# A two-layer decoder step in high and low parts: row sums in a tile of their own, plain blocks' low parts on VectorE, three wide PSUM tiles, and the last projection's first products begun early

## The chip, the cores and the metric

The kernel runs on one core of a Trainium2 chip. The metric is the device time of one execution in microseconds (us). Five engines work in parallel, each through its own instruction stream in order: TensorE (PE; its weight loads are shown as PEld), VectorE (DVE), ScalarE (ACT), GpSimd (POOL) and SyncE (SP, which here only issues DMAs). They meet through semaphores.

## The reference

One inference step of a decoder with two layers on 520 rows of width 1024: 512 prompt rows and 8 rows of samples. Layer 0 mixes tokens by windowed attention, layer 1 by gated linear attention. Behind each stands the same feed-forward block, on which the change bears:

```python
def conv_ffn(x, buf, w_up, conv_w, conv_b, w_down):
    T = x.shape[1]
    h = x @ w_up                                  # 1024 -> 2 * 2816
    a, u = h[..., :D_FF], h[..., D_FF:]
    ap = jnp.concatenate([buf.astype(a.dtype), a], axis=1)
    c = conv_b + sum(conv_w[j] * ap[:, j:j + T] for j in range(CONV_W))   # 3 taps
    y = (jax.nn.gelu(c, approximate=False) * u) @ w_down                  # 2816 -> 1024
    return y, ap[:, T:]
```

## The kernel before

Everything is kept transposed: 128 features on the partitions, rows in the free dimension, in two groups, a (rows 0 to 255) and b (264 rows, the samples among them). Each float32 matrix is split into a high part, rounded by ScalarE to the matmul's type, and a low part, the rest. A product is three matmuls for each 128 features: high by high, high weight by low row, low weight by high row (L216, L218 and L220 or, where all low-weight products come last, L223; L282 to L284 in a pair; L860 to L862 in the partial down projection).

Weights come in units of 128 x 1024 floats (512 KB). SyncE loads the raw unit, ScalarE writes the high part `wh` (L177 in a plain unit). The low part `wl` is made in one of two ways. VectorE subtracts: `wl = raw - wh` (L183, or L288 in `split`). Or, `low_by_dma`: ScalarE writes `-wh` into `wl` (L188) and GpSimd issues a DMA (L189) that loads the unit from memory once more and adds it. Six pairs of `wh` and `wl` slots (`WSLOTS`) and two raw buffers (`RAWS`) go round; a unit's loads are issued in program order when a slot is released.

A feed-forward block has 22 column blocks of 128 gate and 128 value columns. The first four (`PAIRED`) are **plain**: a gate unit and a value unit, each multiplied with the rows of a and of b into one-bank PSUM tiles `accp`, the convolution, the gelu, and `hprod`, the gated product. In the other 18, the **pairs** (`ffn_pair`), gate and value together are computed by a Strassen-like scheme with seven half products instead of eight, on sums and differences of rows (`row_sums`: `th`, `tl`) and of weights. `pair_tasks` prepares the weights in four steps: `upper` loads both raw units and splits one (L245, low part by DMA), `lower` and `sums` add halves on VectorE (L234) and split, `third` splits a half-size sum into `wh3` and `wl3`. `ffn_pair` first makes the product p1 into a one-bank tile `sc`, copies it (L806), then fills three two-bank tiles `widep`, of which VectorE (L799) and ScalarE (L812) make the merged gate and value. Between most pairs stands a unit of the partial down projection (`ffn_down2`), two more wide tiles, which VectorE adds into x (L865, L867). `WIDES` two-bank tiles are there, and four banks for the small tiles (`sc` two of them). The last six blocks' down projection is the ordinary `ffn_down`, eight units, each for a and then for b.

The source gives work in the order of `order()` and `load_next`, which stops while six slots are live, or while two of the `half` tiles are. A scheduler then settles each engine's own sequence, so a matmul can stand far ahead of its place in the source.

Of the kernel before, what the change touches and what calls it, by code (L numbers as in the profile page):

```python
# [11 lines left out]
F32 = mybir.dt.float32  # L12
F32R = mybir.dt.float32r
# [4 lines left out]
PSUM = bass.MemoryType.PSUM  # L18
DRAM = bass.MemoryType.DRAM

P = 128
# [25 lines left out]

PAIRED = 4
ACCS = 4
WIDES = 2  # L50

WARM = 8

# [30 lines left out]
def in_turn(rows):  # L84

    return rows.rearrange("p t j -> p j t")
# [10 lines left out]
class Net:  # L97
    def __init__(self, tc, ctx, I, O):
        self.tc, self.nc, self.I, self.O = tc, tc.nc, I, O
        self.groups = [Group(0), Group(1)]  # L100
        self.stack = ctx
        pool = lambda name, bufs=1, **kw: ctx.enter_context(tc.tile_pool(name=name, bufs=bufs, **kw))
        self.const = pool("const")
        self.act = pool("act")
        self.raw = pool("raw", RAWS)
        self.wts = pool("wts", WSLOTS)
        self.ln = pool("ln")
        self.mps = pool("mps", space=PSUM)
        self.open_acc()
        self.dram = pool("dram", 2, space=DRAM)  # L110
        nc = self.nc
        c = self.const
        self.par = c.tile([P, NPAR], F32, name="par")
        self.ident = c.tile([P, P], F32, name="ident")
        self.ones_a = c.tile([P, P], F32, name="ones_a")
        nc.gpsimd.memset(self.ones_a, 1.0 / D)
        self.eps = c.tile([P, 2], F32, name="eps")
        nc.gpsimd.memset(self.eps[:, 0:1], NORM_EPS)
        nc.gpsimd.memset(self.eps[:, 1:2], 1.0)
        for i, g in enumerate(self.groups):  # L120
            s = [P, KD, g.n]
            g.x = self.act.tile(s, F32, name=f"x_{g.name}")


            if i == 0:
                s = [P, KD, 2, 2, g.n // 2]
                g.xs = self.act.tile(s, F32R, name=f"xs_{g.name}")
                g.hs = self.act.tile(s, F32R, name=f"hs_{g.name}")
                g.xh, g.xl = (g.xs[:, :, :, q] for q in range(2))
                g.hh, g.hl = (g.hs[:, :, :, q] for q in range(2))  # L130
                continue
            s = [P, KD, 2, g.n // 2]
            g.xs = g.hs = None
            g.xh = self.act.tile(s, F32R, name=f"xh_{g.name}")
            g.xl = self.act.tile(s, F32R, name=f"xl_{g.name}")
            g.hh = self.act.tile(s, F32R, name=f"hh_{g.name}")
            g.hl = self.act.tile(s, F32R, name=f"hl_{g.name}")
        self.units = []
        self.w = {}
# [7 lines left out]
    def close(cm):  # L147
        cm.__exit__(None, None, None)

    def open_acc(self):  # L150
        self.acc_cm = self.tc.tile_pool(name="acc", bufs=ACCS, space=PSUM)
        self.acc = self.acc_cm.__enter__()

    def open_wide(self):
        self.acc_cm = self.tc.tile_pool(name="wide", bufs=WIDES, space=PSUM)
        self.acc = self.acc_cm.__enter__()

    def wide(self):
        return self.acc.tile([P, 2, 512], F32, name="widep")


    def load_unit(self, u, pieces=1, late=False):
        src, nt = self.units[u][0], self.units[u][1]
        nc = self.nc
        if nt == 0:
            return self.load_rank(u)
        down = self.units[u][2] == self.ffn_down2
        r = (self.pp if down else self.raw).tile([P, KD * P], F32, name="raw")
        h, l = (self.wts.tile([P, KD * P], F32R, name=name) for name in ("wh", "wl"))
        n = nt * P // pieces  # L170
        for c in (slice(i * n, (i + 1) * n) for i in range(pieces)):
            nc.sync.dma_start(out=r[:, c], in_=src[:, c])
            if late:
                self.spawn(self.parts(u, h[:, c], l[:, c], r[:, c]), 1)
                continue
            if u >= HIACT:
                nc.scalar.activation(h[:, c], r[:, c], AF.Copy)  # L177
            else:
                nc.gpsimd.tensor_scalar(h[:, c], r[:, c], 1.0, 0.0, op0=ALU.mult, op1=ALU.add)
            if self.units[u][2] in (self.ffn_gate, self.ffn_value, self.ffn_down2):  # L180
                self.low_by_dma(l[:, c], h[:, c], src[:, c])
            else:
                nc.vector.tensor_tensor(l[:, c], r[:, c], h[:, c].bitcast(F32), op=ALU.subtract)  # L183
        self.w[u] = (h, l)
# [41 lines left out]
    def pair_tasks(self, u):  # L226


        nc, half = self.nc, KD * P // 2
        lo, hi = slice(0, half), slice(half, KD * P)  # L230
        src0, src1 = self.units[u][0]
        W, T = {}, {}
        self.w[u] = W
        add = lambda o, x, y: nc.vector.tensor_tensor(o, x, y, op=ALU.add)  # L234
        slot = lambda: [self.wts.tile([P, KD * P], F32R, name=name) for name in ("wh", "wl")]

        def keep(h, l, first, second):
            W[first], W[second] = (h[:, lo], l[:, lo]), (h[:, hi], l[:, hi])

        def upper():  # L240
            r1, r0 = (self.raw.tile([P, KD * P], F32, name="raw") for _ in range(2))
            nc.sync.dma_start(out=r1, in_=src1)
            nc.sync.dma_start(out=r0, in_=src0)
            h, l = slot()
            nc.scalar.activation(h, r0, AF.Copy)  # L245
            self.low_by_dma(l, h, src0)
            keep(h, l, "a11", "a12")
            T.update(r0=r0, r1=r1)

        def lower():  # L250
            r0, r1 = T["r0"], T["r1"]
            s = T["s"] = self.pp.tile([P, half], F32, name="sum3")
            add(s, r1[:, lo], r0[:, lo])
            add(r1[:, lo], r1[:, lo], r1[:, hi])
            h, l = slot()
            self.split(h, l, r1)
            keep(h, l, "s1", "a22")

        def sums():
            r0, r1 = T["r0"], T["r1"]  # L260
            add(r0[:, lo], r1[:, lo], r0[:, lo])
            add(r0[:, hi], r0[:, lo], r0[:, hi])
            h, l = slot()
            self.split(h, l, r0)
            keep(h, l, "s2", "s4")

        def third():
            h, l = (self.pp.tile([P, half], F32R, name=name, bufs=2) for name in ("wh3", "wl3"))
            self.split(h, l, T["s"])
            W["s3"] = h, l  # L270

        return [("live", upper), ("live", lower), ("live", sums), ("half", third)]
# [71 lines left out]
    def ln_end(self, g, i, last=False):  # L344
# [72 lines left out]
            self.norm = self.slot + HOLD, self.exp, v.ins, xl.ins, self.next_phase() + 1  # L417
        if i % 2 == 0:
            if g.i:
                self.spawn(self.row_sums(i), 1)  # L420
            return
        for m in range(KD):
            yield 1 if m else LATEB
# [6 lines left out]
    def row_sums(self, i):  # L430
# [11 lines left out]
            v.tensor_tensor(self.t1[k], a.x[:, k, 0:256], b.x[:, k, 0:256], op=ALU.subtract)  # L442
            self.shift(b, i, half + k)
        yield 1
        r = wide(self.raw.tile([P, KD * P], F32, name="raw"))
        for k in range(half):
            v.scalar_tensor_tensor(r[:, k], self.t1[k], -1.0, b.x[:, half + k, 0:256], op0=ALU.mult, op1=ALU.subtract)
            self.shift(a, i, half + k)
# [330 lines left out]
    def ffn_pair(self, u, layer, j, q):  # L779
# [4 lines left out]
        if j == PAIRED:  # L784
            self.row_sum1()
            self.close(self.cp_cm)
            self.cp, self.cp_cm = self.open(f"merged{layer}")
            self.m = [self.cp.tile([P, 2, 2 + NT], F32, name=f"merged{i}") for i in range(2)]
            self.c = [self.cp.tile([P, 2, NT - 256], F32, name=f"conv{i}") for i in range(2)]
            for t in self.m:  # L790
                nc.gpsimd.memset(t[:, 0, 0:2], 0.0)
            self.close(self.acc_cm)
            self.open_wide()
        half = KD // 2
        part = lambda g, ks: (g.xh[:, ks], g.xl[:, ks])
# [4 lines left out]
        M, C = self.m[j % 2], self.c[j % 2]  # L800
        both = lambda x: x.unsqueeze(1).broadcast_to([P, 2, x.shape[-1]])
        g, h = M[:, 0], M[:, 1, 2:]
        p1 = self.mtile("sc")
        self.half_product(p1, W["a11"], part(a, lo), n)
        v = self.ln.tile([P, NT - 256], F32, name="nv")[:, :n]
        nc.scalar.copy(v, p1[:, :n])  # L806
# [32 lines left out]
        if j == NF - 1:  # L839
            nc.scalar.dma_start(out=self.O["conv_p"][layer], in_=self.nconv_p)  # L840
            nc.scalar.dma_start(out=self.O["conv_s"][layer], in_=self.nconv_s)
            for cm in (self.cp_cm, self.pp_cm, self.fp_cm, self.acc_cm):
                self.close(cm)
            self.open_acc()

    def ffn_down2(self, u, layer, part, i):
# [20 lines left out]
                nc.vector.tensor_tensor(x, x, ps[:, :, :n], op=ALU.add)  # L867
        self.release()

    def ffn_down(self, g, u, layer, part, m):  # L870
        nc = self.nc
        ps = self.product(g, u, g.hh, g.hl)
        yield from self.ln_chunk(g, m, ps, True, last=layer == 1)
        if m == KD - 1:
            yield from self.ln_end(g, 2 * layer + 1, last=layer == 1)
# [340 lines left out]
    def load_next(self):  # L1216
        while True:
# [9 lines left out]
            if kind == "live":  # L1227
                if self.live == WSLOTS:
                    return
                self.live += 1  # L1230
            else:
                if self.half == 2:
                    return
                self.half += 1
            self.todo.pop(0)
# [6 lines left out]
    def run(self):  # L1242
# [20 lines left out]
        while self.later:  # L1263
            self.slot += 1
            self.due()
        self.close(self.acc_cm)


def build(nc, I, O):
# [115 lines left out]
```

## Time and profile before

| | |
|---|---|
| timed runs | 1193.8 us median of 2 (1192.94 and 1194.66) |
| profiled execution | 1184.46 us, span of the trace 1182.7 us |
| PE busy | 1095.6 us (93%), 9174 matmuls |
| DVE, ACT, POOL busy | 896.1 (76%), 657.5 (56%), 356.2 us (30%) |
| mean granted PE clock | 0.973 of full |
| feed-forward block of layer 0: plain blocks, pairs | 187 to 235 us, 235.5 to 504.5 us of the span |
| feed-forward block of layer 1: plain blocks, pairs | 810 to 857.7 us, 857.7 to 1128.7 us |

In a row of the chain of waits stand the engine, the line that waited, what it waited for, the total in us, how often, and the longest. In a row of the timeline stand the start in us, the duration in us, the engine, the line, the operation, the tile written, the tiles read, and in brackets the idle time ahead of the row and what ended it. A row of windows has, for each stretch, the busy us and the number of instructions of each engine, then the granted PE clock, the DMA engines' busy share and GB/s.

### The profile page before, as it was taken

The page shows a single profiled execution, that of the slowest core. Times are in us where ns is not written, and L with a number is a line of the kernel's source. Part 1 is how long each engine was busy: PE and PEld are TensorE (multiplying, and loading weights), DVE is VectorE, ACT ScalarE, POOL GpSimd, SP SyncE. Part 2 cuts the span into 40 slices and gives each one's busy share as a digit, 9 for nine tenths or more (in the row PEclk, how much of TensorE's full clock was granted, in tenths as well). Part 3 has the DMA queues.
Part 4 walks back from the last instruction along what each step waited for, and adds up shares of the span by engine and source line. Part 5 has one row for each costly group of instructions (what it writes and reads, how often), then busy time and mean ns, then how long its engine had stood idle before and what let it go on. Part 6 is the DMA issues. An engine that isn't in the chain of part 4 may idle for free. (4 is left out here: it accounts for less than half of the span.)

```text
span 1182.7 us, 23889 instructions
## 1 busy us (share of the span) xinstructions
PE 1095.6 (93%) x9174; PEld 1055.4 (89%) x9174; DVE 896.1 (76%) x1778; ACT 657.5 (56%) x1307; POOL 356.2 (30%) x565
## 2 busy tenths in 40 slices
PE   9999996899999999999999999997799999999995
PEld 8997895899999999988899999996799999999995
DVE  7897678667777777778867877778657877777776
ACT  5677456656555565445545655455655556555444
POOL 3575677211111111056211100467211111111045
PEclk9999998999999999999899999997989999999998
DMA  7562132766677776432125355331767777776412
GB/s 237 154 189 67 50 100 49 161 167 167 171 164 170 169 165 155 128 106 91 54 99 164 106 174 179 130 119 43 165 160 166 164 165 163 178 171 150 132 55 73
DMA packets 64466, 161.68 MB, mean 137 GB/s; under 512 B 7992, under 2 KB 28512, under 8 KB 64352
## 3 DMA queue, kind: packets, MB, share of 16 engines
q1 hardware_dynamic: 51536, 119.47, 31.7%
q0 software_dynamic: 10656, 38.80, 19.6%
q10 hardware_dynamic: 2160, 1.89, 0.5%
q8 instruction: 72, 1.18, 0.4%
q14 instruction: 42, 0.34, 0.1%
HBM read 147.47 MB, written 8.47 MB: 132 GB/s over the span
## 5 line engine op out<-in xcount | busy, mean ns | idle before, releaser
L177 ACT ACTIVATE wh<-raw 128x1024 fp32r<-128x1024 f32 (+2 forms) x98 | 99.3, 1013 | 79.9 <-PE widep L283 41.4
L189 POOL DMA_DIRECT2D wl<-in_w_down x32 | 27.6, 863 | 345.8 <-ACT wl L188 345.8
L216 PE MATMUL accp<-xs_a,wh 128*128 128x256 f32 x400 | 113.5, 298 | 10.9 <-ACT wh L177 9.5
L282 PE MATMUL widep<-th,wh 128*128 128x264 f32 (+1 forms) x432 | 120.0, 278 | 0.0
L283 PE MATMUL widep<-tl,wh 128*128 128x264 f32 (+1 forms) x432 | 119.9, 278 | 0.0
L284 PE MATMUL widep<-th,wl 128*128 128x264 f32 (+1 forms) x432 | 119.8, 277 | 0.0
L216 PE MATMUL accp<-xh_b,wh 128*128 128x264 f32 x400 | 115.6, 289 | 4.1 <-ACT xh_b L413 4.1
L220 PE MATMUL accp<-xh_b,wl 128*128 128x264 f32 x400 | 113.5, 284 | 0.0
L218 PE MATMUL accp<-xl_b,wh 128*128 128x264 f32 x384 | 108.5, 283 | 0.0
L218 PE MATMUL accp<-xs_a,wh 128*128 128x256 f32 x384 | 107.7, 293 | 0.0
L288 DVE TENSOR_TENSOR wl<-raw,wh 128x1024 fp32r<-128x1024 f32 x72 | 86.7, 1220 | 10.4 <-ACT wh L287 10.1
L216 PEld LDWEIGHTS accp<-xs_a,wh 128*128 128x128 f32 x400 | 81.6, 205 | 13.1 <-ACT wh L177 10.4
L183 DVE TENSOR_TENSOR wl<-raw,wh 128x1024 fp32r<-128x1024 f32 (+3 forms) x64 | 74.9, 1176 | 11.5 <-ACT wh L177 11.0
L216 PEld LDWEIGHTS accp<-xh_b,wh 128*128 128x128 f32 x400 | 77.5, 194 | 6.4 <-ACT xh_b L413 4.9
L282 PEld LDWEIGHTS widep<-th,wh 128*128 128x128 f32 x432 | 83.0, 192 | 0.0
L283 PEld LDWEIGHTS widep<-tl,wh 128*128 128x128 f32 x432 | 83.0, 192 | 0.0
L284 PEld LDWEIGHTS widep<-th,wl 128*128 128x128 f32 x432 | 82.9, 192 | 0.0
L287 ACT ACTIVATE wh<-raw 128x1024 fp32r<-128x1024 f32 x72 | 74.2, 1046 | 13.2 <-PE accp L218 5.8
L282 PE MATMUL widep<-xh_b,wh 128*128 128x264 f32 x288 | 79.8, 277 | 0.0
L283 PE MATMUL widep<-xl_b,wh 128*128 128x264 f32 x288 | 79.6, 277 | 0.0
L284 PE MATMUL widep<-xh_b,wl 128*128 128x264 f32 x288 | 79.6, 277 | 0.0
L218 PEld LDWEIGHTS accp<-xs_a,wh 128*128 128x128 f32 x384 | 78.4, 204 | 1.1 <-DVE xs_a L288 0.7
(410 smaller groups left out, 4263.7 us busy)
## 6 DMA issues: line engine op xcount, KB each, us to landing
raw<-in_w_up SPq DMA_DIRECT2D x88, 512.0 KB, 4.2
wl<-in_w_up POOLq DMA_DIRECT2D x42, 512.0 KB, 6.4
raw<-in_w_down SPq DMA_DIRECT2D x32, 512.0 KB, 4.1
wl<-in_w_down POOLq DMA_DIRECT2D x32, 512.0 KB, 6.4
raw<-in_w_gla SPq DMA_DIRECT2D x24, 512.0 KB, 3.5
raw<-in_w_mix_o SPq DMA_DIRECT2D x16, 512.0 KB, 4.4
raw<-in_w_down SPq DMA_DIRECT2D x16, 384.0 KB, 3.3
qs<-hl SPq DMA_DIRECT2D x64, 64.0 KB, 2.2
```

The lines of the kernel that those rows point to most:

```text
L177: nc.scalar.activation(h[:, c], r[:, c], AF.Copy)
L183: nc.vector.tensor_tensor(l[:, c], r[:, c], h[:, c].bitcast(F32), op=ALU.subtract)
L189: self.nc.gpsimd.dma_start(out=l, in_=src, accum_op=ALU.add)
L216: nc.tensor.matmul(o, h[:, ks], xh, start=k == 0, stop=False)
L218: nc.tensor.matmul(o, h[:, ks], xl, start=False, stop=False)
L220: nc.tensor.matmul(o, l[:, ks], xh, start=False, stop=not tail and k == nt - 1)
L282: self.nc.tensor.matmul(o, h[:, ks], rh, start=k == 0, stop=False)
L283: self.nc.tensor.matmul(o, h[:, ks], rl, start=False, stop=False)
L284: self.nc.tensor.matmul(o, l[:, ks], rh, start=False, stop=k == KD // 2 - 1)
L287: self.nc.scalar.activation(hi, src, AF.Copy)
L288: self.nc.vector.tensor_tensor(lo, src, hi.bitcast(F32), op=ALU.subtract)
```

## The change

- The raw tile of a plain unit is always one of the two of the pool `raw`. The difference of rows `r` in `row_sums`, and `r0` of `upper`, move into tiles `raw` of the pool `pp`, two of their own; `upper` issues the load of `r0` first. `row_sums` starts three slots later in place of one.
- Low parts of gate and value units are subtracted by VectorE; only `upper` and `ffn_down2` keep the DMA. Of the units that take this path, three in each layer, six negations on ScalarE and six DMAs of 512 KB on GpSimd's queue go, and six VectorE subtractions of 128x1024 come.
- `WIDES` is 3. The small tiles' banks are closed during the pairs, and p1 has two banks of its own, `onep`.
- `wh3` and `wl3` have one buffer in place of two, and `half` stops at one.
- The last down projection's first four products for a are begun together over their first five 128-feature steps (`HEADS`), and ended one by one.

```diff
-WIDES = 2
+WIDES = 3
+HEADS = 4
...
     def open_wide(self):
-        self.acc_cm = self.tc.tile_pool(name="wide", bufs=WIDES, space=PSUM)
-        self.acc = self.acc_cm.__enter__()
+        self.acc, cm0 = self.psum("wide", WIDES)
+        self.one, cm1 = self.psum("one", 2)
+        self.psum_cms = cm1, cm0
...
-        down = self.units[u][2] == self.ffn_down2
-        r = (self.pp if down else self.raw).tile([P, KD * P], F32, name="raw")
+        r = self.raw.tile([P, KD * P], F32, name="raw")
...
-            if self.units[u][2] in (self.ffn_gate, self.ffn_value, self.ffn_down2):
+            if self.units[u][2] == self.ffn_down2:
                 self.low_by_dma(l[:, c], h[:, c], src[:, c])
             else:
                 nc.vector.tensor_tensor(l[:, c], r[:, c], h[:, c].bitcast(F32), op=ALU.subtract)
...
         def upper():
-            r1, r0 = (self.raw.tile([P, KD * P], F32, name="raw") for _ in range(2))
+            r0 = self.pp.tile([P, KD * P], F32, name="raw", bufs=2)
+            r1 = self.raw.tile([P, KD * P], F32, name="raw")
+            nc.sync.dma_start(out=r0, in_=src0)
             nc.sync.dma_start(out=r1, in_=src1)
-            nc.sync.dma_start(out=r0, in_=src0)
...
-            h, l = (self.pp.tile([P, half], F32R, name=name, bufs=2) for name in ("wh3", "wl3"))
+            h, l = (self.pp.tile([P, half], F32R, name=name) for name in ("wh3", "wl3"))
...
-                self.spawn(self.row_sums(i), 1)
+                self.spawn(self.row_sums(i), 3)
...
-        r = wide(self.raw.tile([P, KD * P], F32, name="raw"))
+        r = wide(self.pp.tile([P, KD * P], F32, name="raw", bufs=2))
...
-        p1 = self.mtile("sc")
+        p1 = self.one.tile([P, 512], F32, name="onep")
...
     def ffn_down(self, g, u, layer, part, m):
-        ps = self.product(g, u, g.hh, g.hl)
+        end = self.units[u][1] - 1
+        if g.i == 0 and m == 0:
+            self.heads = [self.acc.tile([P, 512], F32, name="accp") for _ in range(HEADS)]
+            for i, ps in enumerate(self.heads):
+                self.down_steps(g, u + i, ps, range(end))
+        if g.i == 0 and m < HEADS:
+            ps = self.heads[m]
+            self.down_steps(g, u, ps, [end])
+            ps = ps[:, :g.n]
+        else:
+            ps = self.product(g, u, g.hh, g.hl)
...
-                if self.half == 2:
+                if self.half == 1:
```

`down_steps` issues the three matmuls of `product` for each of the given 128-feature steps.

The change moves instructions on the engines. In the rows below, those of after bear the changed file's line numbers: L177 is L186 there, L183 is L192, L188 is L197, L234 is L243, L245 is L255, L282 to L284 are L292 to L294, L287 and L288 are L297 and L298, L767 is L777, L799 is L809, L806 is L816, L812 is L822 and L829 is L839.

First, ScalarE where the plain blocks of layer 0 begin: `aext` and `conv` belong to the convolution, `th` is the high part of the row sums, `wh` and `wl` are the parts of the next plain unit. Before:

```order
L754 COPY aext<-accp 128x264
L767 ACTIVATE conv<-conv 128x256
L756 ACTIVATE conv<-accp,par 128x256
L287 ACTIVATE th_2735<-raw 128x8x128
L177 ACTIVATE wh<-raw 128x1024
L287 ACTIVATE hs_a<-hprod 128x2x128
L767 ACTIVATE conv<-conv 128x264
L188 ACTIVATE wl<-wh 128x1024
```

After:

```order
L764 COPY aext<-accp 128x264
L777 ACTIVATE conv<-conv 128x256
L766 ACTIVATE conv<-accp,par 128x256
L186 ACTIVATE wh<-raw 128x1024
L297 ACTIVATE th_2734<-raw 128x8x128
L297 ACTIVATE hs_a<-hprod 128x2x128
L777 ACTIVATE conv<-conv 128x264
```

The high part of the weights now stands ahead of the row sums' first split, and the negation is gone.

Second, PE in the pairs of layer 0, with tile numbers, around p1 of the fourth pair (`sc_3974` before, `onep_3975` after: the same product). Before, these are rows 1783 to 1788 of the engine's sequence:

```order
L283 MATMUL widep_3796<-tl0_2738,wh_3618 128x264
L284 MATMUL widep_3796<-th0_2735,wl_3619 128x264
L284 MATMUL sc_3974<-xs_a_86,wl_3692 128x256
L282 MATMUL sc_3974<-xs_a_86,wh_3691 128x256
L283 MATMUL sc_3974<-xs_a_86,wh_3691 128x256
L284 MATMUL sc_3974<-xs_a_86,wl_3692 128x256
```

After, these are rows 1877 to 1881:

```order
L872 MATMUL widep_3942<-hl_b_92,wh_3694 128x264
L873 MATMUL widep_3942<-hh_b_91,wl_3695 128x264
L292 MATMUL onep_3975<-xs_a_86,wh_3704 128x256
L293 MATMUL onep_3975<-xs_a_86,wh_3704 128x256
L294 MATMUL onep_3975<-xs_a_86,wl_3705 128x256
```

Before, p1 is cut up and stands between the wide tiles of the pair ahead of its own; after, its twelve matmuls stand together at the head of their own pair, behind the partial down projection. The first matmul on the low part `wl_3692` is row 1785 before, and on the same part (`wl_3705`) row 1881 after.

Third, ScalarE in the pairs, where that low part is made, from the copy of the first wide tile of the second pair on (`widep_3603` before, `widep_3604` after). Before:

```order
L812 COPY merged1_3386<-widep_3603 128x8
L177 ACTIVATE wh_3666<-raw_3665 128x1024
L806 COPY nv_3794<-sc_3781 128x256
L188 ACTIVATE wl_3667<-wh_3666 128x1024
L245 ACTIVATE wh_3691<-raw_3688 128x1024
L188 ACTIVATE wl_3692<-wh_3691 128x1024
L287 ACTIVATE wh3_3815<-sum3_3774 128x512
L829 ACTIVATE conv1_3388<-merged1_3386,par_78 128x512
```

After:

```order
L822 COPY merged1_3383<-widep_3604 128x8
L186 ACTIVATE wh_3694<-raw_3693 128x1024
L197 ACTIVATE wl_3695<-wh_3694 128x1024
L255 ACTIVATE wh_3704<-raw_3700 128x1024
L297 ACTIVATE wh3_3689<-sum3_3582 128x512
L197 ACTIVATE wl_3705<-wh_3704 128x1024
L839 ACTIVATE conv1_3385<-merged1_3383,par_78 128x512
```

The upper unit is split at the same place; `wh3` now stands between its high part and its negation, and is the third pair's, where it was the fourth's. With one buffer it waits for the last matmul on the `wh3` before it (row 1697 of PE's sequence, in the third wide tile of the second pair; the first one, `widep_3604`, fills rows 1627 to 1650).

More of the change, by code (lines that the diff above doesn't have):

```diff
@@ L107, in __init__ @@
         self.ln = pool("ln")
-        self.mps = pool("mps", space=PSUM)
         self.open_acc()
@@ L148, in close, with psum, close_psum @@
         cm.__exit__(None, None, None)
+    def psum(self, name, bufs=1):
+        cm = self.tc.tile_pool(name=name, bufs=bufs, space=PSUM)
+        return cm.__enter__(), cm
     def open_acc(self):
-        self.acc_cm = self.tc.tile_pool(name="acc", bufs=ACCS, space=PSUM)
-        self.acc = self.acc_cm.__enter__()
+        self.mps, cm0 = self.psum("mps")
+        self.acc, cm1 = self.psum("acc", ACCS)
+        self.psum_cms = cm1, cm0
     def open_wide(self):
-        self.acc_cm = self.tc.tile_pool(name="wide", bufs=WIDES, space=PSUM)
-        self.acc = self.acc_cm.__enter__()
+        self.acc, cm0 = self.psum("wide", WIDES)
+        self.one, cm1 = self.psum("one", 2)
+        self.psum_cms = cm1, cm0
+    def close_psum(self):
+        for cm in self.psum_cms:
+            self.close(cm)
     def wide(self):
@@ L791, in ffn_pair @@
                 nc.gpsimd.memset(t[:, 0, 0:2], 0.0)
-            self.close(self.acc_cm)
+            self.close_psum()
             self.open_wide()
@@ L841, in ffn_pair @@
             nc.scalar.dma_start(out=self.O["conv_s"][layer], in_=self.nconv_s)
-            for cm in (self.cp_cm, self.pp_cm, self.fp_cm, self.acc_cm):
+            for cm in (self.cp_cm, self.pp_cm, self.fp_cm):
                 self.close(cm)
+            self.close_psum()
             self.open_acc()
@@ L868, in ffn_down2, with down_steps @@
         self.release()
-    def ffn_down(self, g, u, layer, part, m):
-        nc = self.nc
-        ps = self.product(g, u, g.hh, g.hl)
+    def down_steps(self, g, u, ps, ks):
+        nc = self.nc
+        h, l = self.w[u]
+        o, end = ps[:, :g.n].rearrange("p (j t) -> p j t", t=2), self.units[u][1] - 1
+        for k in ks:
+            w = slice(k * P, k * P + P)
+            rh, rl = in_turn(g.hh[:, k]), in_turn(g.hl[:, k])
+            nc.tensor.matmul(o, h[:, w], rh, start=k == 0, stop=False)
+            nc.tensor.matmul(o, h[:, w], rl, start=False, stop=False)
+            nc.tensor.matmul(o, l[:, w], rh, start=False, stop=k == end)
+    def ffn_down(self, g, u, layer, part, m):
+        end = self.units[u][1] - 1
[9 more added lines that the diff above has]
+            ps = self.product(g, u, g.hh, g.hl)
         yield from self.ln_chunk(g, m, ps, True, last=layer == 1)
@@ L1265, in run @@
             self.due()
-        self.close(self.acc_cm)
+        self.close_psum()
 def build(nc, I, O):
```

## The prediction, on record before the run

> **What bounds the kernel now.** I read the page first, then the chain of waits of TensorE, then stretches of the span, then the timeline at the waits.
>
> ```profile
> PE 1095.6 (93%) x9174; PEld 1055.4 (89%) x9174; DVE 896.1 (76%) x1778; ACT 657.5 (56%) x1307; POOL 356.2 (30%) x565
> ```
>
> TensorE has the work; no other engine is near its limit over the whole. The same 9174 matmuls are issued after the change, so whatever is gained comes out of TensorE's waits and its slow clock. The chain of waits of that engine says for whom it waits:
>
> ```profile
> PE sc L284 <- DMA wl<-in_w_up: 15.6, 15, 1.7
> PE accp L216 <- ACT wh L177: 9.5, 4, 4.2
> PE widep L282 <- DVE hprod L775: 9.2, 2, 5.1
> PE accp L223 <- DMA wl<-in_w_up: 7.0, 2, 4.0
> PE accp L216 <- DVE merged L799: 4.2, 2, 2.1
> PE widep L860 <- DVE merged L799: 2.8, 4, 1.2
> ```
>
> Four of the rows lie in the feed-forward blocks' openings or at their ends (twice each, once a layer, L177 in the main), two in the pairs. The stretches give the size of each place (layer 0's plain blocks, its pairs, layer 1's pairs):
>
> ```profile
> 187.00:235.00 48.00, 34.72 (x246) 32.36 (x245) 34.15 (x69) 27.99 (x49) 22.92 (x36) 0.86 0.50 112
> 235.50:504.50 269.00, 259.42 (x2265) 256.91 (x2266) 203.25 (x339) 151.08 (x219) 37.24 (x67) 0.99 0.67 162
> 857.70:1128.70 271.00, 261.28 (x2266) 258.32 (x2266) 203.02 (x339) 150.89 (x219) 37.76 (x67) 0.99 0.67 160
> ```
>
> **Pairs: the low part that comes by DMA.** Without a wait one matmul follows another every 0.112 us: from the first to the sixth of these rows, 0.56 us in five steps. Then the engine stands.
>
> ```profile
> 268.91 0.28 PE L282 MATMUL widep<-th,wh 128*128 128x264 f32 x1
> ...
> 269.47 0.28 PE L284 MATMUL widep<-th,wl 128*128 128x264 f32 x1
> 270.48 0.38 PE L284 MATMUL sc<-xs_a,wl 128*128 128x256 f32 x1 [0.73 <-DMA wl<-in_w_up]
> ```
>
> 2266 matmuls at 0.112 are 253.8 us; the stretches are 269.0 and 271.0, so 15.2 and 17.2 us are lost. Part of it is slow clock:
>
> ```profile
> 191.40:201.40 10.00, 5.91 (x22) 5.11 (x23) 7.96 (x16) 5.98 (x9) 9.97 (x14) 0.50 0.17 53
> 208.50:211.70 3.20, 3.20 (x15) 3.20 (x16) 0.21 (x1) 1.15 (x3) 0.18 (x1) 0.50 1.07 268
> 235.80:239.00 3.20, 3.20 (x17) 3.20 (x17) 0.43 (x1) 1.01 (x2) 0.13 (x2) 0.50 0.90 256
> 857.90:863.70 5.80, 5.80 (x28) 5.80 (x29) 2.03 (x3) 1.18 (x2) 0.13 (x2) 0.50 0.46 137
> ```
>
> The first two rows belong to the opening, below. In the last two, at a clock of 0.50, 17 matmuls took 3.2 us (1.3 too much) and 28 took 5.8 us (2.7 too much). These stand behind the opening's last wait, which stays. That leaves 13.9 and 14.5 us of waits, 28.4 together, of which the first and the last row of waits name 15.6 and 2.8; the rest are steps too short for that list.
>
> Why is the low part late? The chain behind the wait at 270.48, on ScalarE and GpSimd:
>
> ```profile
> 260.80 1.06 ACT L245 ACTIVATE wh<-raw 128x1024 fp32r<-128x1024 f32 x1 [0.64 <-DMA raw<-in_w_up]
> 261.89 1.07 ACT L188 ACTIVATE wl<-wh 128x1024 fp32r<-128x1024 f32 x1
> ...
> 263.25 0.86 POOL L189 DMA_DIRECT2D wl<-in_w_up  x1 [1.93 <-ACT wl L188]
> ```
>
> From the high part to the landing it takes 270.4 less 260.8, 9.6 us, and 7.2 of them lie behind the issue. That doesn't change. What changes is when the part is asked for: the first matmul on it is row 1785 of PE's sequence before and row 1881 after, while the split stands behind the same copy of the same wide tile. 96 rows are 10.8 us. The longest wait in the list is 1.7 us, so all 15 should go, with 9 us to spare.
>
> Two things eat of that margin. Behind the split, `wh3` now stands ahead of the negation, and with one buffer it waits for row 1697. The negation and `low_by_dma` stand behind it, as does L829, which needs the third wide tile anyway. From row 1697 to row 1881 are 184 rows, 20.6 us; `wh3` (0.6 us), the negation (1.07) and issue to landing (7.2) are 8.9. It holds with 11 us. `wh3` itself is asked for 122 rows later, 13.7 us, and in the pairs without a down unit 72 matmuls, 8.1 us, after its buffer is free, against 0.61 and 0.68 us for the two halves of its split (ScalarE and VectorE, by the rows below). Bounds of the single buffer: nothing, or 1.3 us in each of 36 pairs, 47 us, if nothing hid it; I take nothing, since both leads are over six times the split.
>
> ```profile
> L287 ACT ACTIVATE wh<-sum 128x512 fp32r<-128x512 f32 x16 | 9.8, 614 | 0.0
> L288 DVE TENSOR_TENSOR wl<-sum,wh 128x512 fp32r<-128x512 f32 x16 | 10.9, 683 | 0.0
> L799 DVE TENSOR_TENSOR conv<-widep,merged 128x512 f32<-128x512 f32 x18 | 12.4, 691 | 24.1 <-PE widep L284 24.1
> ```
>
> The third wide tile gives VectorE a tile's time more (24 matmuls, 2.7 us) to read the one before it; in the last row VectorE waits for TensorE 24.1 us in this stretch, and it is busy for 203 of 269. It can take back the 2.8 us of the last row of waits, or nothing; by their place both of a layer's are the down unit behind a merge, so I count them as gone. Of the 28.4 us I leave 3 for the shortest steps, 0.1 us each, which I can't trace to a cause: **25.5 us**. Bounds: 14 (half stays) and 28.4.
>
> **Openings.** Layer 0, around the second and third plain unit:
>
> ```profile
> 194.02 0.56 ACT L756 ACTIVATE conv<-accp,par 128x256 f32<-128x256 f32 x1
> 195.29 1.14 ACT L287 ACTIVATE th<-raw 128x1024 fp32r<-128x1024 f32 x1 [0.71 <-DVE raw L447]
> 196.32 1.05 ACT L177 ACTIVATE wh<-raw 128x1024 fp32r<-128x1024 f32 x1
> 197.43 0.58 PE L216 MATMUL accp<-xs_a,wh 128*128 128x256 f32 x1 [4.09 <-ACT wh L177]
> ...
> 208.38 1.22 PE L223 MATMUL accp<-xs_a,wl 128*128 128x256 f32 x4 [4.01 <-DMA wl<-in_w_up]
> ```
>
> `wh` stands behind the row sums' `th`, which waits for VectorE. After, it stands ahead of it: it can begin at 194.6 and end at 195.6, so TensorE goes on **1.8 us** earlier. The low part then comes from VectorE, 1.3 us behind it (below), long before TensorE has done the high products: the wait of **4.0 us** is gone, and with it the slow stretch behind it, 15 matmuls in 3.2 us, **1.5**. Against this: the slow clock of the first stall lasts past 201.4 in any case (the row from 191.40), so starting 1.8 earlier puts some eight matmuls more into it (0.9), and the next unit's low part, third in VectorE's queue, comes some 0.6 late. Layer 0: 1.8 + 4.0 + 1.5 - 0.9 - 0.6 = **5.8 us**. In layer 1 the chain of waits of that stretch (810 to 858 us) has the same two, and no slow stretch follows the second: 1.8 + 3.0 - 0.9 = **3.9**.
>
> ```profile
> PE accp L216 <- ACT wh L177: 4.2, 1, 4.2
> PE accp L223 <- DMA wl<-in_w_up: 3.0, 1, 3.0
> ```
>
> On the price of it bear these rows:
>
> ```profile
> L183 DVE TENSOR_TENSOR wl<-raw,wh 128x1024 fp32r<-128x1024 f32 x42 | 53.8, 1283 | 7.4 <-ACT wh L177 6.9 <-PE accp L220 0.3
> L188 ACT ACTIVATE wl<-wh 128x1024 fp32r<-128x1024 f32 x74 | 78.1, 1055 | 0.7
> 196.59 1.69 POOL L428 TENSOR_SCALAR x_a<-x_a,par 128x256 f32<-128x256 f32 x1
> 196.80 1.21 DVE L288 TENSOR_TENSOR tl<-raw,th 128x1024 fp32r<-128x1024 f32 x1
> 200.86 0.48 POOL L428 TENSOR_SCALAR x_b<-x_b,par 128x264 f32<-128x264 f32 x1
> ```
>
> That is six VectorE subtractions of 1.28 us, three a layer, for six negations of 1.06 us and six issues of 0.86 us. VectorE is busy 34 of 48 us there, and TensorE waits at the end for its `hprod`: 0 to 7.7 us in all. There is more to it: GpSimd's shift of one x chunk took 1.69 us beside VectorE's subtraction of 1.21 us, and 0.48 us while VectorE stood idle. The difference is the subtraction. So each of the six can hold GpSimd's shifts by 1.2 us, and the row sums read them.
>
> The Trainium skill, "SBUF — State Buffer", section "Who interferes with whom", says the same as a rule: a VectorE instruction with two inputs in SBUF and a GpSimd one that reads SBUF share a port, and one waits for the other. By that rule the low part on VectorE is no gift; the trace agrees, 1.69 against 0.48 us.
>
> I take nothing for this in the sum, as GpSimd loses 3 x 0.86 us of issues a layer in the same stretch, and it is a rival. TensorE's last wait of the opening (the row `hprod`, 9.2 us) stays: before, 14 matmuls of p1 had been taken ahead of it; after, p1 stands behind it, which at an unchanged `hprod` makes the wait longer by 14 x 0.112 = 1.6 us a layer. Against it, the negation of 1.06 us that leaves ScalarE's queue ahead of the last gelu, and the last units' matmuls that are no longer held by a low part. I take **0**, bounds -3.2 and +1.
>
> **Ends.** The wait for `merged` (2.1 us a layer) stands ahead of the last down projection. The scheduler had already mixed its first four products, 60 matmuls in the same order before and after; the first still needs the last wide tile to be read. VectorE's queue up to that read (L799, the second row) was two low parts and this 0.69 us; after, it is two low parts and two splits of 0.41 and 0.47 us (L288 on `hs_a` and `hl_b`).
>
> ```profile
> 504.22 0.69 DVE L836 SCALAR_TENSOR_TENSOR merged<-conv,merged 128x520 f32<-128x520 f32 x1
> ...
> 505.70 1.03 DVE L799 TENSOR_TENSOR merged<-widep,conv 128x528 f32<-128x528 f32 x2
> 506.65 0.41 DVE L288 TENSOR_TENSOR hs_a<-merged,hs_a 128x256 fp32r<-128x256 f32 x1
> 506.98 0.47 DVE L288 TENSOR_TENSOR hl_b<-merged,hh_b 128x264 fp32r<-128x264 f32 x1
> ```
>
> I take **0** for both layers; bounds -0.4 and 4.2, the whole wait.
>
> **Sum.** 25.5 + 5.8 + 3.9 + 0 + 0 = 35.2 us. The profiled execution took 1184.46 us (span 1182.7), which becomes 1149.3. The timed runs' median is 1193.8, 9.3 us more, for a reason the trace can't show; I let it stand and predict 1193.8 - 35.2 = 1158.6, rounded to **1159 us**, 2.9% less. What a measurement of this kernel tells from no change is about 2%, 23.9 us: 1169.9.
>
> The clock decides some of it. After a stall of over 4 us the granted clock was 0.50 for 3.2 us and more; after the stalls of 1 to 1.9 us in the pairs it was not. So the waits removed from the pairs bring no clock, and are worth their own length.
>
> The Trainium skill, "TensorE: Matmul & The Clock Gate", section "Part 1: The HAM clock gate", has a free-running window of about 3.4 us that has to be idle for the half clock; by it the loss of the opening can fall anywhere from none to two windows. The trace agrees in the length (3.2 us and multiples); it would shift the sum by some 2 us either way.
>
> **Rivals.**
>
> 1. *The pairs' waits only change hands.* Once TensorE no longer waits for the DMA, VectorE's reads of the wide tiles come to the same engine closer together: 203 us of work in 269 less 14, 80% busy, in one queue in order. If half of the 28.4 us comes back as waits for `merged`, `conv` or x, the gain is 14.2 + 9.7 = 24 us, **1170**; if all, 1184. For it: the row of waits for `merged`. Against: the tile's time more, and VectorE's 24.1 us of idling for TensorE.
> 2. *The openings bring nothing*: shifts held by the six subtractions (7.4 us) and p1 behind `hprod` (3.2) eat their 9.7. Gain 25, **1168**.
> 3. *The low part is late after all, and slower.* Place: the first low product of p1, with nothing in front of it to hide behind, as all of its pair stands behind it. Price: each us by which split, `wh3`, negation, issue and landing exceed 20.6 us from row 1697 costs 36 us over the 36 pairs. It eats the gain at 21.6 and loses 2% at 22.3 us (1.0 and 1.7 more, 35.2 and 59.1 by 36). If raw load (the row below), both splits, `wh3`, both negations and both accumulations of a cycle ran one after the other, 4.2 + 2.1 + 0.6 + 2.1 + 2 x 7.2 = 23.4 us, that would be 1159 + 36 x 2.8 = **1260**. Against: the raw tile of its own, loaded first, and 8.9 us as the sum of its own rows.
>
> ```profile
> raw<-in_w_up SPq DMA_DIRECT2D x88, 512.0 KB, 4.2
> ```
>
> 4. *It doesn't do what it says.* The order shows that it does, but for the heads, which are priced at nothing.
>
> **How the numbers follow.** Forecast, 1148 to 1167: 0.60. Rival 1: 0.20, nearly half of it below 1169.9. Rival 2: 0.12, most of it below. Rival 3: 0.05, and no change from other causes 0.03. Faster by over 2%: 0.60 + 0.09 + 0.08, lowered to 0.72 for what no row shows; within: 0.22; slower: 0.06. The low end is the 28.4 us whole, the ends at 4.2, and what I took off the openings (0.9 + 0.6 + 0.9) given back: 1159 - 2.9 - 4.2 - 2.4 = 1149.5, and 1148 for the gap between executions. The high end takes in rival 2 and rival 1 up to three quarters, 1170 + 7 = 1177.
>
> **What would show it.** Right: no row of p1 waiting for the DMA in the pairs; both stretches of pairs at about 256 to 258 us; no wait of L223 for a DMA; the wait for `hprod` still there, 4 to 6 us a layer. Wrong: p1 waiting for `wl` (rival 3), wide tiles waiting for VectorE's `merged`, `conv` or x by more than 5 us (rival 1), waits for `hprod` above 15 us in all (rival 2).

## The result, and the profile after

The changed kernel took 1148.18 us, median of two runs (1146.55 and 1149.82), against 1193.8: a ratio of 0.962 (95% interval 0.955 to 0.968). The forecast was 1159 us and its range 1148 to 1177; the time lies 0.2 us inside the low end, and one of the two runs lies below it. On two later chips the same kernel stood at 0.966 (0.963 to 0.969) and 0.968 (0.965 to 0.970) of the kernel before. The profiled execution took 1149.82 us, span 1148.1; span against span, 34.6 us less. Three later executions, of three different kernels, took 1250, 3866 and 4742 us and are left out of all numbers here.

From the page after, the engines, columns as before:

```profile
PE 1085.6 (95%) x9174; PEld 1049.6 (91%) x9174; DVE 896.0 (78%) x1784; ACT 650.6 (57%) x1301; POOL 352.7 (31%) x559
```

The chain of waits of TensorE; these rows answer to the six shown of before:

```profile
PE onep L292 <- DVE hprod L785: 15.7, 2, 9.9
PE accp L225 <- ACT wh L186: 6.0, 4, 2.2
PE accp L888 <- DVE merged L809: 3.5, 2, 1.8
PE accp L229 <- DVE wl L192: 3.2, 4, 1.4
```

No row of p1 or of a wide tile waits for a DMA or for `merged`, and L232 (L223 before) waits for no DMA. Of the last row 0.6 us is the low part of a plain unit, which now comes from VectorE; the rest lies outside the plain blocks, where before a like row (L220 for the `wl` of L183) had 2.6 us. In the two stretches of pairs TensorE has no wait at all that the list shows. The stretches, with p1's 12 matmuls in front (2280 matmuls, which at 0.112 us are 255.4):

```profile
230.90:489.40 258.50, 258.46 (x2280) 258.49 (x2280) 202.49 (x343) 152.23 (x223) 32.01 (x67) 0.99 0.70 166
837.80:1095.00 257.20, 257.17 (x2280) 257.18 (x2280) 202.60 (x343) 152.39 (x223) 32.11 (x67) 0.99 0.69 167
```

TensorE is busy through all of each; before, stretches of 269.0 and 271.0 us had 259.4 and 261.3 us of work. But the wait for `hprod` ahead of them is larger, 15.7 us for 9.2 (15.0 and 14.8 in the two later profiles of the same kernel). Between the starts of the same-numbered matmuls of both traces, in us:

| | before | after |
|---|---|---|
| up to the out projection of layer 0 | 164.2 | 165.6 |
| rest of it, plain blocks, pairs of layer 0 | 339.3 | 322.6 |
| wait at the end | 2.4 | 2.1 |
| last down projection, linear attention | 277.9 | 278.7 |
| rest of the out projection, plain blocks, pairs of layer 1 | 344.0 | 324.8 |
| wait at the end | 2.4 | 1.9 |
| last down projection | 40.3 | 40.3 |

### The profile page after: what moved, and what is told of

Read it like the earlier page. It is cut to its first block, busy times and chain, and to the rows that moved or that the text cites. A ratio compares the mean times of both kernels' runs of the same rounds, so it can differ in the third digit from the quotient of the medians.

```text
span 1148.1 us, 23839 instructions
## 1 busy us (share of the span) xinstructions
PE 1085.6 (95%) x9174; PEld 1049.6 (91%) x9174; DVE 896.0 (78%) x1784; ACT 650.6 (57%) x1301; POOL 352.7 (31%) x559
## 4 chain that ended last, share of the span: by engine, by line
PE 63%; DVE 16%; DMA 6%; POOL 5%; ACT 5%; issue 3%; SPq 0%; ACTq 0%; DVEq 0%; POOLq 0%
PE widep L292 8%; PE widep L293 8%; PE widep L294 8%; PE widep L873 5%; PE widep L872 5%; PE widep L871 5%; PE accp L227 4%; PE accp L225 4%; PE accp L229 4%; DMA vb<-dv 2%; PE onep L292 1%; PE onep L294 1%; PE onep L293 1%; DVE wl L192 1%; DMA raw<-in_w_up 1%
## 5 line engine op out<-in xcount | busy, mean ns | idle before, releaser
L297 ACT ACTIVATE wh<-raw 128x1024 fp32r<-128x1024 f32 x72 | 76.4, 1061 | 117.7 <-PE widep L872 84.3
L198 POOL DMA_DIRECT2D wl<-in_w_down x32 | 27.4, 858 | 348.2 <-ACT wl L197 348.2
L186 ACT ACTIVATE wh<-raw 128x1024 fp32r<-128x1024 f32 (+2 forms) x98 | 99.1, 1012 | 59.5 <-PE accp L227 21.6
L292 PE MATMUL widep<-th,wh 128*128 128x264 f32 (+1 forms) x432 | 119.2, 276 | 0.0
L294 PE MATMUL widep<-th,wl 128*128 128x264 f32 (+1 forms) x432 | 119.2, 276 | 0.0
L298 DVE TENSOR_TENSOR wl<-raw,wh 128x1024 fp32r<-128x1024 f32 x72 | 87.9, 1222 | 24.2 <-ACT wh L297 24.2
L192 DVE TENSOR_TENSOR wl<-raw,wh 128x1024 fp32r<-128x1024 f32 (+3 forms) x70 | 82.0, 1178 | 10.6 <-ACT wh L186 9.9
L809 DVE TENSOR_TENSOR merged<-widep,conv 128x528 f32<-128x528 f32 x72 | 37.4, 560 | 65.4 <-PE widep L294 65.4
L292 PEld LDWEIGHTS widep<-th,wh 128*128 128x128 f32 x432 | 82.3, 190 | 0.0
L294 PEld LDWEIGHTS widep<-th,wl 128*128 128x128 f32 x432 | 82.2, 190 | 0.0
L292 PE MATMUL widep<-xh_b,wh 128*128 128x264 f32 x288 | 79.6, 276 | 0.0
```

Of the source, the lines that this page charges most:

```text
L292: self.nc.tensor.matmul(o, h[:, ks], rh, start=k == 0, stop=False)
L294: self.nc.tensor.matmul(o, l[:, ks], rh, start=False, stop=k == KD // 2 - 1)
L297: self.nc.scalar.activation(hi, src, AF.Copy)
L298: self.nc.vector.tensor_tensor(lo, src, hi.bitcast(F32), op=ALU.subtract)
```

## The experiments

The change falls into three parts that can stand alone: the low parts, the PSUM part and the raw tiles (with `wh3`, `half` and the row sums' start). The first theory, the prediction's, was that p1's place in PE's sequence makes nearly all of the pairs' gain.

**Each part alone.** The kernel before, with one part each.

```diff
# low parts
-            if self.units[u][2] in (self.ffn_gate, self.ffn_value, self.ffn_down2):
+            if self.units[u][2] == self.ffn_down2:
```

> The kernel before, with the low parts of the plain gate and value units on VectorE as the only edit. Theory (the openings gain by the low part, and TensorE's wait for hprod takes part of it back; the pairs gain only by where p1 stands): the two waits of L223 for a DMA, 7.0 us, go; both stretches of pairs stay at 269 to 271 us with some 15 waits of sc for the DMA; the whole is 3 to 8 us faster, ratio 0.993 to 0.998. Rival (the six subtractions hold GpSimd's shifts and the row sums): the wait for hprod grows by as much as L223 gives, ratio 1.000 or above.

Measured: ratio 0.995 (0.993 to 0.997), 6 us, as forecast. The waits of `sc` stay (15.8 us, 17 of them), and the wait for `hprod` grows from 9.2 to 11.8 us.

```diff
# PSUM part
-WIDES = 2
+WIDES = 3
...
+        self.acc, cm0 = self.psum("wide", WIDES)
+        self.one, cm1 = self.psum("one", 2)
...
-        p1 = self.mtile("sc")
+        p1 = self.one.tile([P, 512], F32, name="onep")
...
```

> The kernel before, with the PSUM part of the change as the only edit: three two-bank tiles and p1 in a pool of two banks of its own. Theory: p1 then stands whole at the head of its pair, the low part is asked for 96 matmuls later, and the pairs lose all their waits for a DMA: both stretches (2280 matmuls with p1) at 257 to 259 us, the wait for hprod larger by 3 to 4 us in all, the opening's waits for wh (8 us) and for wl by DMA (7 us) unchanged: 22 to 27 us faster on the profile, ratio 0.975 to 0.982. Rival (r0 in its own buffer and loaded first makes the low part early): without that the waits for the DMA stay, at least half, ratio 0.99 to 1.00.

Measured: ratio 0.997 (0.995 to 0.999), 3 us: a miss by 20 us. No wait for the DMA is left, so the step from p1's place to the low part was right. But its chain of waits of TensorE has others:

```profile
PE onep L291 <- DVE hprod L784: 11.2, 2, 5.6
PE accp L225 <- DVE merged L808: 10.1, 2, 5.7
PE accp L225 <- ACT wh L186: 8.7, 3, 4.1
PE accp L232 <- DMA wl<-in_w_up: 8.0, 2, 4.2
PE widep L870 <- ACT merged L821: 4.8, 14, 0.6
```

The wait for `merged` at the ends has gone from 4.2 to 10.1 us, and 14 small waits for the copy of 8 columns in the pairs are new. VectorE's own chain of waits in most of layer 0's pairs (240 to 480 us) tells why; first before, then with the PSUM part alone:

```profile
DVE sum L234 <- DMA raw<-in_w_up: 24.7, 16, 2.7
```

```profile
DVE sum L243 <- DMA raw<-in_w_up: 41.2, 16, 3.8
```

VectorE stands in each pair until the raw units have landed, with the reads of the wide tiles behind it in its queue. Before, TensorE's wait for the low part hid that. The raw units are late because both come into the pool of two raw buffers, which the pair before frees late. In the timeline of this kernel's SyncE, and of its VectorE:

```profile
394.21 0.33 SPq L251 DMA_DIRECT2D raw<-in_w_up  x1
396.14 0.33 SPq L252 DMA_DIRECT2D raw<-in_w_up  x1
```

```profile
394.89 1.23 DVE L297 TENSOR_TENSOR wl<-raw,wh 128x1024 fp32r<-128x1024 f32 x1
...
400.31 0.69 DVE L243 TENSOR_TENSOR sum<-raw 128x512 f32<-128x512 f32 x1 [2.73 <-DMA raw<-in_w_up]
```

The split of the pair before, which reads the raw unit, ends at 396.12; the load is issued at 396.14, and VectorE goes on at 400.31. So a second limit stood behind the first one.

```diff
# raw tiles
-            r1, r0 = (self.raw.tile([P, KD * P], F32, name="raw") for _ in range(2))
+            r0 = self.pp.tile([P, KD * P], F32, name="raw", bufs=2)
+            r1 = self.raw.tile([P, KD * P], F32, name="raw")
...
-                if self.half == 2:
+                if self.half == 1:
```

Not shown here are four edits of the same part: r0 loaded first, the row sums' own tile and later start, the single buffers of `wh3` and `wl3`, and the raw unit of the partial down projection, which had its one tile in `pp` and now takes one of the pool `raw`. (It is this unit, and not a plain one, that the first point of the change moves; a plain unit's raw tile was in `raw` already.) So four raw buffers serve the pairs where three did.

> The kernel before, with the raw tiles as the only edit: row sums' difference and r0 in tiles of their own, r0 loaded first, one buffer for wh3 and wl3, half at one, row sums three slots later. Theory: p1 stays cut up between the wide tiles of the pair ahead, so the waits of sc for the DMA stay (10 to 16 us) and only the openings' wait for wh gets shorter, by 3 to 4 us: ratio 0.994 to 1.000. Rival (the raw buffers made the low part late): the waits of sc for the DMA fall below 5 us, ratio 0.98 to 0.99.

Measured: ratio 0.996 (0.994 to 0.998), 5 us, as forecast. Here VectorE waits for no raw unit in that stretch, and TensorE still for the low part, even more:

```profile
PE sc L284 <- DMA wl<-in_w_up: 18.9, 18, 1.9
```

**Two parts each.** The new theory is two limits in a row: p1's place makes TensorE wait for the low part, the raw buffers make VectorE wait for raw units, and each hides the other. Then either of these two parts, with low parts on VectorE but without the other, should give next to nothing, and the two together nearly all. The first of the three expectations below was written before this theory.

```diff
# both, the low parts by DMA as before (the changed kernel with one line back)
-            if self.units[u][2] == self.ffn_down2:
+            if self.units[u][2] in (self.ffn_gate, self.ffn_value, self.ffn_down2):
```

> The changed kernel, with the low parts of plain units by DMA again as the only edit. Theory: pairs stay without waits (257 to 259 us each), the wait of L223 for the DMA is back with 5 to 8 us, and the wait for hprod (15.7 us in the changed kernel) falls by a part of it: 2 to 6 us slower than the changed kernel, ratio to the kernel before 0.964 to 0.972. Rival (the subtractions cost the openings as much as the DMA did): as fast as the changed kernel or faster, 0.962 or below.

Measured: 1156.91 us, ratio 0.974 (0.971 to 0.977). The PSUM part and the raw tiles together give 30 us, alone 3 and 5. The wait of L232 for the DMA is back, and the wait for `hprod` smaller:

```profile
PE onep L292 <- DVE hprod L785: 10.3, 2, 5.2
PE accp L232 <- DMA wl<-in_w_up: 9.6, 2, 6.3
```

So the low parts on VectorE are worth about 8 us beside the other two parts, a little over the 2 to 6 forecast; the changed kernel wasn't run on that chip, so this stands on its times on other chips. By the starts of the same-numbered matmuls in the two profiles, some 6 us of it lie in layer 0's plain blocks and some 3 in layer 1's out projection.

Next, the change without the raw tiles (the kernel before with the first two diffs):

> The changed kernel without its raw tiles: the kernel before with the PSUM part and the low parts on VectorE, and raw tiles, wh3 and half as before. Theory (two limits in a row: p1's place makes TensorE wait for the low part, and the two raw buffers make VectorE wait for r1 and r0, which shows once the first is gone): VectorE waits about 40 us for raw loads in each stretch of pairs, the stretches take 262 to 264 us, the ends' wait for merged is 4 to 6 us a layer; ratio 0.985 to 0.992. Rival (the raw tiles matter only in the openings): pairs at 257 to 259 us, ratio below 0.975.

Measured: ratio 0.990 (0.987 to 0.994). In its pairs VectorE waits for raw units, and its ends wait for `merged`:

```profile
DVE sum L243 <- DMA raw<-in_w_up: 39.0, 16, 3.8
```

```profile
PE accp L225 <- DVE merged L808: 9.7, 2, 5.5
```

And the change without the PSUM part (the first and the third diff):

> The changed kernel without its PSUM part: the kernel before with the raw tiles and the low parts on VectorE. Theory (two limits in a row in the pairs, p1's place and the raw buffers; taking one away leaves the other): sc waits for the DMA 15 to 19 us, VectorE waits for no raw load in the pairs, ratio 0.988 to 0.995, about the product of the two edits alone (0.9962 and 0.9952: 0.991). Rival (the low parts and raw tiles carry the gain and p1's place only helps in the end): ratio below 0.98.

Measured: ratio 0.990 (0.987 to 0.993), by the product of the two alone 0.991. VectorE waits for no raw unit in the pairs, TensorE for the low part:

```profile
PE sc L284 <- DMA wl<-in_w_up: 20.8, 15, 2.0
```

Both ratios are as the theory of two limits had them.

**The order of the loads.** The raw tiles' part also loads r0 first.

```diff
+            nc.sync.dma_start(out=r1, in_=src1)
             nc.sync.dma_start(out=r0, in_=src0)
-            nc.sync.dma_start(out=r1, in_=src1)
```

> The changed kernel with r1 loaded ahead of r0, as before the change, r0 still in its own buffer. Theory (the buffer counts, not the order; the low part has 11 us to spare): within 0.3% of the changed kernel. Rival (the order counts, as r0 now queues on SyncE behind r1, which waits for a raw buffer): VectorE or TensorE waits again in the pairs, 5 us or more slower than the changed kernel.

Measured: 1149.0 us, ratio 0.967 (0.965 to 0.970); the changed kernel on that chip had 1149.29, 0.968. The order is worth nothing. The other edits of this part (the buffers, `half`, the row sums' start) were not run one by one; that the raw buffers count rests on the traces, where a load is issued as a buffer comes free.

> The changed kernel again, beside the next three on one chip: ratio to the kernel before 0.955 to 0.968.

**The heads.**

```diff
-        if g.i == 0 and m == 0:
+        if False and g.i == 0 and m == 0:
...
-        if g.i == 0 and m < HEADS:
+        if False and g.i == 0 and m < HEADS:
```

> The changed kernel without the heads: the last down projection's first products in the source's plain order. Theory (the scheduler had mixed them before): same sequence on every engine, so within 0.1% of the changed kernel, and the wait for merged at the ends 1.7 to 1.9 us a layer. Rival (the heads gave the ends something): 2 to 4 us slower than the changed kernel.

> The changed kernel once more, on the chip on which the next three run, to compare with them: ratio to the kernel before 0.955 to 0.968, no wait for a DMA in the pairs on TensorE or VectorE.

Measured: 1149.30 us against 1149.07 on the same chip, both 0.966. The heads are worth nothing: every engine's sequence in the trace is the same with and without them. The wait for `merged` is 3.4 us here and 3.5 in the changed kernel.

**The wait for `hprod`.** It is the largest that is left. Two things make it long. After the change, p1 and the first wide tile lie in banks that the plain blocks' products held, so p1 itself waits. And VectorE, which makes `hprod`, stands for a raw unit in the opening; in the changed kernel's timeline, layer 1, SyncE and VectorE:

```profile
814.41 0.33 SPq L181 DMA_DIRECT2D raw<-in_w_down  x1
815.64 0.33 SPq L252 DMA_DIRECT2D raw<-in_w_up  x1
819.27 0.33 SPq L253 DMA_DIRECT2D raw<-in_w_up  x1
```

```profile
813.17 1.22 DVE L192 TENSOR_TENSOR wl<-raw,wh 128x1024 fp32r<-128x1024 f32 x1
...
818.01 1.23 DVE L298 TENSOR_TENSOR wl<-raw,wh 128x1024 fp32r<-128x1024 f32 x1
...
826.84 0.69 DVE L243 TENSOR_TENSOR sum<-raw 128x512 f32<-128x512 f32 x1 [5.96 <-DMA raw<-in_w_up]
...
837.26 0.42 DVE L785 TENSOR_TENSOR hprod<-conv,accp 128x264 f32<-128x264 f32 x1
```

With the low part's DMA at 817.71, four transfers of 512 KB go from 814.4 to 826.8 us, 2.1 MB in 12.4 us. The load of the down unit (L181) is issued as VectorE's first subtraction here ends (814.39), that of r1 (L253) as the second ends (819.24): both come from the pool of two raw buffers and wait for one. The first try gives p1 and the first wide tile other banks, which the small tiles held (`wide` then takes the three pools in turn):

```diff
-        self.acc, cm0 = self.psum("wide", WIDES)
-        self.one, cm1 = self.psum("one", 2)
+        self.one, cm = self.psum("one", 2)
+        opened = [self.psum(f"wide{i}") for i in range(WIDES)]
```

> The changed kernel with p1's two banks opened first and each wide tile in a pool of its own, so that p1 and the first wide tile take banks that the plain blocks' products don't hold: 38 matmuls stand ahead of the first wait for hprod where none did. Theory (TensorE's wait at the first pair is for the banks that hprod still reads): the wait for hprod falls from 15.7 to 7 or 8 us in all, 8 us faster than the changed kernel, ratio to the kernel before lower by 0.006 to 0.007. Rival (the first wide tile's own weights come late from VectorE, which waits for a raw load): the wait moves to th or wl there, 0 to 4 us faster.

Measured: 1137.56 us, ratio 0.958 (0.954 to 0.961), 11.5 us less than the changed kernel on that chip, where 8 were forecast: the wait fell by 8.4 us from that chip's profile of the changed kernel (15.0), and the mean granted clock rose from 0.973 to 0.981, which the forecast had not counted. The wait is down to this, while VectorE still stands 5.8 us for the raw unit in layer 1:

```profile
PE widep L294 <- DVE hprod L787: 6.6, 2, 5.4
```

The second try, on top, loads the first unit of the partial down projection behind the next pair's r0 and r1, where it had stood ahead of them:

```diff
+                if self.units[u][2] == self.ffn_down2 and self.units[u][3][1:] == (0, 0):
+                    self.todo = self.pair_tasks(u + 1)
+                    self.todo[1:1] = one
+                    self.nu += 1
```

> The kernel with p1's banks first, and in it the first partial-down unit of each layer loaded behind the fifth block's... next pair's raw units instead of ahead of them. Theory (in the opening VectorE stands 2 and 5.8 us for the raw unit r1, since four transfers of 512 KB share the DMA engines; one of them moved behind brings r1 some 3 us earlier, and hprod with it): the wait for hprod falls from 6.6 to 2 to 4 us, 2 to 5 us faster than the kernel with p1's banks first, ratio 0.953 to 0.956. Rival (r1 waits for its raw buffer and not for the DMA engines): no change, or slower by up to 2 us as the down unit comes later.

Measured: 1132.25 us, ratio 0.954 (0.951 to 0.956), 17.0 us less than the changed kernel on that chip. No row of `hprod` is left in TensorE's chain of waits, and of VectorE's stall in layer 1's opening this:

```profile
DVE sum L245 <- DMA raw<-in_w_up: 1.0, 1, 1.0
```

The rival of this expectation had a share in it. SyncE in layer 1's opening, with the first try and then with the second (L183 loads the down unit, L254 r0, L255 r1):

```profile
806.00 0.33 SPq L183 DMA_DIRECT2D raw<-in_w_down  x1
807.20 0.33 SPq L254 DMA_DIRECT2D raw<-in_w_up  x1
810.84 0.33 SPq L255 DMA_DIRECT2D raw<-in_w_up  x1
```

```profile
806.29 0.33 SPq L255 DMA_DIRECT2D raw<-in_w_up  x1
807.51 0.33 SPq L254 DMA_DIRECT2D raw<-in_w_up  x1
811.14 0.33 SPq L183 DMA_DIRECT2D raw<-in_w_down  x1
```

Loaded behind, the down unit also leaves the first free raw buffer to r1, whose load is issued about 4.5 us earlier. How much of the gain is this and how much the transfers that no longer stand ahead of r1 was not separated.

## Why the prediction was right, and where not

**What bounds the kernel** was read rightly: the gain came out of TensorE's waits, which fell where they were named, but for `hprod`. The clock was read rightly too: the mean granted clock is 0.973 before and after, so the waits taken out of the pairs brought none.

**Pairs.** Predicted 25.5 us. By the stretches with p1's 14 or 12 matmuls (before 269.0 and 271.0 plus 1.6 each, after 258.4 and 257.1, by the matmuls' starts 12.2 and 15.5 less) it is 27.7. The size was right and its reason only half. The step that failed is the one that gave it all to the 96 rows by which p1 is asked for later, with the raw tile of its own as a mere margin: that step alone left VectorE's wait for raw units, 41 us in the 240 us looked at. The prediction had looked at VectorE's 24.1 us of idling for TensorE and took it for slack. It hadn't looked at what VectorE itself waits for. Rival 1, waits that change hands, is what happens with the PSUM part alone; the raw tiles keep it from happening. Rival 3 was not seen anywhere: no low part of a pair came late in the changed kernel, and `wh3` with its one buffer waited 0.6 us in those 240.

**Openings.** Predicted 5.8 + 3.9 + 0. Of the rows named, the wait of L223 for a DMA went (7.0 us) and the wait for `wh` fell from 9.5 to 6.0. The wait for `hprod`, taken at 0 with bounds -3.2 and +1, grew by 6.5. That term was mis-sized: 3.1 us are p1's lost cover, which the text had and then set off against a negation; the rest goes with VectorE's stall for a raw unit, which it didn't have. That stall grew by 3.6 us. VectorE's waits in the openings of layer 0 and 1, before and then after:

```profile
DVE sum L234 <- DMA raw<-in_w_up: 2.1, 1, 2.1
DVE sum L234 <- DMA raw<-in_w_up: 3.0, 1, 3.0
```

```profile
DVE sum L243 <- DMA raw<-in_w_up: 2.7, 1, 2.7
DVE sum L243 <- DMA raw<-in_w_up: 6.0, 1, 6.0
```

The two terms fit the other profiles of the same sequence. In all of them the wait for `hprod` is the stall and 7.0 to 7.2 us more (15.7 with a stall of 8.7, 15.0 with 7.9, 14.8 with 7.8, and 11.7 with 4.5 in the run without heads); before, it was the stall of 5.1 and 4.1 more, and 4.1 and 3.1 are 7.2. The low parts on VectorE pay here for a part of what they bring: in each of four pairs of kernels that differ by them alone this wait is longer with them, 11.8 us for 9.2, 19.6 for 11.2, 9.9 for 7.6, and 15.7 for 10.3. By the prediction's own sign, over 15 us in all, rival 2 was just present in this wait (15.7), though not at its full price: together the openings had 4.0 us less of waits, for 9.7 predicted.

By the starts of the same-numbered matmuls the plain blocks are 3.2 us shorter in layer 0 and 0.8 in layer 1, the same 4.0. Layer 1's out projection, which the sum didn't have, was 3.6 us shorter. It takes 27.4 to 27.9 us, between the same two matmuls, in the eight profiles with raw tiles and low parts on VectorE, and 28.9 to 31.0 in the six others; by which wait was not traced.

**GpSimd's shifts** were held by the subtraction, as rival 2 had it: the four shifts of x_a take 4.55 us after, 3.49 before (GpSimd's timeline of before, then of after).

```profile
194.78 3.49 POOL L428 TENSOR_SCALAR x_a<-x_a,par 128x256 f32<-128x256 f32 x4
```

```profile
196.20 4.55 POOL L438 TENSOR_SCALAR x_a<-x_a,par 128x256 f32<-128x256 f32 x4
```

No longer wait is seen for it: VectorE's wait for GpSimd there is 1.8 us after and was 1.7. Low parts by DMA again cost about 8 us, so moving them paid.

**Ends.** Predicted 0, measured 0.7 us for both; the heads nothing, as said.

**The sum.** 35.2 us predicted for the profile, 34.6 measured between spans. That they lie so close is luck: the openings gave 5.7 us less than forecast and the pairs 2.2 more, layer 1's out projection and the ends 4.3 that the sum didn't have, and by the table 2.2 us were lost ahead of layer 0's out projection and between the two layers' blocks. The medians moved by 45.6, since the kernel before had been profiled in one of its quicker executions: over the later runs it took 1182 to 1196 us, and the changed kernel 1146 to 1151. On the two later chips the gain was 38 to 40 us. Letting the 9.3 us between profile and median stand on both sides was the other step that failed; the changed kernel's own profile lay within its runs. Whether the waits for a DMA make the kernel before vary more was not tested.

## What to carry to other kernels

Where two limits stand one behind the other, each removed alone shows next to nothing: here 3 and 5 us alone, 30 together. Before an edit is priced by the waits of the busiest engine, look at the waits of the engine that will be late next, and at what stands ahead of it in that queue. And when a pool's banks change hands between two phases, the first tiles of the new phase belong in the banks that came free first: with a load moved behind a more urgent one, that gave 17 us more.

## What the runs showed of the hardware that was not expected

Four transfers of 512 KB took 12.4 us in the opening of layer 1, where one took 3.6 us to land at the median: less than four times that (14.4). With a load that is needed late issued a few us ahead of one that is needed at once, VectorE stood 5.8 us for the latter, and 1.0 with the order changed; the first of the two also took the raw buffer that came free first.
